# Add and GELU on one core: GpSimd instead of ScalarE waits for the last store at the program's end

## The chip, the core and the metric

The kernel runs on one core of a Trainium2 chip. The metric is the device time of one execution in microseconds, as the median of several runs. Beside the runs there is one profiled execution; its rows, clocked from the first instruction of the program, are what is read below.

## What is computed

```python
def setup_inputs():
    batch, dim = 1024, 4096
    return {
        "x": np.random.randn(batch, dim).astype(np.float32),
        "y": np.random.randn(batch, dim).astype(np.float32),
    }

def reference(x, y):
    z = x + y
    return (0.5 * z * (1 + np.tanh(np.sqrt(2 / np.pi) * (z + 0.044715 * z ** 3)))).astype(np.float32)
```

Two matrices of 16 MiB each are read, added and passed through the tanh form of GELU; one matrix of 16 MiB is written.

## The kernel before

Each of the 128 partitions holds 8 rows of 4096, which are 32768 values in a row. The loads are two of x (16384 values a partition each, L125) and four of y (8192 each, L132). All transfers are issued by SyncE (SP) on one queue. The arithmetic goes in 16 chunks of 2048: the sum z = x + y is made by GpSimd (10 chunks) or VectorE (6 chunks), both at L149; ScalarE takes the magnitude of z (L154) and the GELU of its negative (L157) into PSUM; VectorE adds max(z, 0) and writes z back (L166). Three stores of 16384, 10240 and 6144 values a partition (L136) follow the loads in SP's queue. The order on each engine is written out by hand (L173 to L209).

After the program has been compiled, two functions edit its instruction lists. `begin_early` (L9) moves the first two loads ahead of the barrier at the program's start. `wait_late` (L23) works on the last block of the program, which every program of this kind has. In that block stand, in order:

1. SP's waits for everything that is still under way (`all_done`, L30);
2. a first barrier of all five engines: each adds one to a gather semaphore, GpSimd waits for four, takes them off and releases the other four engines;
3. GpSimd's `reset`, a drain, and the clearing of the program's semaphores (`clear`, L33, issued at L47 as ranges);
4. a second barrier of the same form.

`wait_late` takes the wait for the semaphore of the last store out of SP's waits (L40 to L43), leaves that one semaphore out of the cleared ranges (L44 to L49), and appends one instruction to the very end of the block (L50 to L63): it waits until the semaphore has reached 32 (16 for the first load of y, 16 for the last store, which share it) and subtracts 32. So barriers and clearing run while the last store is still being written, and one engine waits for the store at the end. Lines of the inserted code carry the numbers L47 and, for the rest of the end block, L213 in the profile, which is the line where the program was finished.

```python
    end.append(
        mybir.InstEventSemaphore(
            name=clear.name, engine=mybir.EngineType.Activation, debug=clear.debug,
            sync_info=mybir.SyncInfo(
                on_wait=[its],
                on_update=[
```

Of the kernel before, what the change touches and what calls it, by code (L numbers as in the profile page):

```python
# [22 lines left out]
def wait_late(nc):  # L23

    body, end = (b.instructions for b in nc.main_func.blocks[1:3])
    last = [i for i in body if isinstance(i, mybir.InstDMACopy)][-1]
    (sem,) = [u.id for u in last.sync_info.on_update]
    all_done = end[0]  # L30
    reset = next(i for i in end if isinstance(i, mybir.InstDrain) and i.is_reset_sema)
    at = end.index(reset)
    clear = end[at + 1]  # L33
    first, stop = reset.reset_range_start, reset.reset_range_stop
    assert all_done.engine == mybir.EngineType.SP and reset.engine == mybir.EngineType.Pool
    assert isinstance(clear, mybir.InstISA) and clear.engine == mybir.EngineType.Pool
    waits = all_done.sync_info.on_wait
    (its,) = [w for w in waits if w.id == sem]

    end[0] = mybir.InstDrain(  # L40
        name=all_done.name, engine=all_done.engine, debug=all_done.debug, is_reset_sema=False,
        sync_info=mybir.SyncInfo(on_wait=[w for w in waits if w.id != sem], on_update=[]),
    )  # L43
    parts = []  # L44
    for f, e in ((first, sem), (sem + 1, stop)):
        if f < e:
            nc.gpsimd.sem_clear(range(f, e))  # L47
            parts.append(nc.cur_bb.bb.instructions.pop())
    end[at + 1 : at + 2] = parts  # L49
    end.append(  # L50
        mybir.InstEventSemaphore(
            name=clear.name, engine=mybir.EngineType.Activation, debug=clear.debug,
            sync_info=mybir.SyncInfo(
                on_wait=[its],
                on_update=[
                    mybir.SyncUpdate(
                        sync_type="semaphore", id=sem, ant_name=its.ant_name,
                        update_mode="sem-sub-imm", update_value=its.wait_value,
                    )
                ],  # L60
            ),
        )
    )  # L63
# [3 lines left out]
def kernel(  # L67
# [145 lines left out]
    tc.compile()  # L213
    begin_early(nc, 2)
    wait_late(nc)


# [28 lines left out]
```

## Time and profile before

| what | us |
|---|---|
| median of 3 runs | 120.06 (120.06 to 120.14) |
| span of the profiled execution, first to last instruction of the program | 118.57 (118.6 on the page) |
| median less span | 1.49 |
| last store issued by SP | 107.56 |
| its landing, issue to last of 16 completions | 11.0 |
| busy: VectorE, ScalarE, GpSimd | 59.8, 60.8, 55.5 |
| busy share of the DMA queue's packets | 98.6% of 16 engines |

The profiled execution's own device time is not among the times shown; its span and the records of semaphores around it are. The span ends with ScalarE's instruction at the end of the block. What lies after it is no part of the kernel's code: the trace has there only updates of semaphores by the frame in which every program runs, the last of them 120.18 us after the first instruction.

In the profile, an engine's name with a q (ACTq, POOLq) is its sequencer: instructions that wait, count or branch, and keep no arithmetic unit busy. Semaphore instructions are shown with the time at which their wait was met, not the time at which the wait began. An update is the moment at which a semaphore's value changes.

### The profile page before, as it was taken

The numbers are of one execution on the slowest core, as the hardware profiler recorded it, in microseconds if no ns is written. First come the engines' busy times: TensorE is split into PE (matmuls) and PEld (weight loads), VectorE is DVE, ScalarE is ACT, GpSimd is POOL, SyncE is SP. The second block draws the span as 40 slices with busy tenths as digits, with TensorE's granted clock in tenths as the row PEclk, the third lists the DMA queues.
The fourth block names the chain that finished last, engine by engine and source line by source line (L and its number), as shares of the span: only waits on it lengthen the run. The fifth ranks groups of instructions, "written<-read, shape, count | busy, mean of one in ns | idle before, by whom it ended". The sixth has DMA issues, their size and how long they took to land.

```text
span 118.6 us, 160 instructions
## 1 busy us (share of the span) xinstructions
DVE 59.8 (50%) x24; ACT 60.8 (51%) x34; POOL 55.5 (47%) x14
## 2 busy tenths in 40 slices
DVE  0000000000399999699994594257999457742000
ACT  5000000000067979999379705797798999940000
POOL 0000000000399999997000029999999999100000
DMA  7989888998889988988899898998899889999996
GB/s 243 464 365 696 354 354 354 663 398 354 354 387 497 531 354 354 707 354 354 354 420 464 365 520 354 531 531 354 354 531 531 354 354 442 442 442 442 398 398 265
DMA packets 1296, 50.33 MB, mean 424 GB/s; under 512 B 144, under 2 KB 144, under 8 KB 144
## 3 DMA queue, kind: packets, MB, share of 16 engines
q1 hardware_dynamic: 1296, 50.33, 98.6%
HBM read 33.55 MB, written 16.78 MB: 424 GB/s over the span
## 4 chain that ended last, share of the span: by engine, by line
DMA 48%; POOL 34%; POOLq 4%; ACT 3%; DVE 2%; issue 0%; SPq 0%; DVEq 0%
POOL z L149 34%; DMA z<-in_x_dram 26%; DMA y<-in_y_dram 21%; POOLq L213 4%; DVE z L166 2%; ACT w L154 2%; ACT w L157 2%; SPq L132 0%; POOLq L149 0%; DVEq L166 0%
## 5 line engine op out<-in xcount | busy, mean ns | idle before, releaser
L149 POOL TENSOR_TENSOR z<-z,y 128x2048 f32<-128x2048 f32 x10 | 55.3, 5563 | 45.6 <-DMA z<-in_x_dram 31.1
L154 ACT ACTIVATE w<-z 128x2048 f32<-128x2048 f32 x16 | 30.1, 1880 | 42.5 <-DVE z L149 36.0
L166 DVE SCALAR_TENSOR_TENSOR z<-z,w 128x2048 f32<-128x2048 f32 (+1 forms) x17 | 36.4, 2157 | 16.0 <-ACT w L157 16.0
L149 DVE TENSOR_TENSOR z<-z,y 128x2048 f32<-128x2048 f32 x6 | 24.0, 4009 | 30.3 <-DMA z<-in_x_dram 30.1
L157 ACT ACTIVATE w<-w 128x2048 f32<-128x2048 f32 x16 | 29.8, 1862 | 0.5
L198 ACT ACT_TABLE_LOAD x1 | 1.3, 1283 | 1.3 <-PEq L230 1.3
L197 DVE MEMSET one<- 128x1 f32 x1 | 0.1, 59 | 1.3 <-PEq L230 1.3
L198 ACT ACTIVATE one<-one 128x1 f32<-128x1 f32 x1 | 0.2, 203 | 0.0
L230 POOL MEMSET const-float32-0.0<- 128x1 f32 x1 | 0.1, 98 | 0.2 <-issue 0.2
L230 POOL MEMSET const-bfloat16-1.0<- 128x1 bf16 x1 | 0.1, 101 | 0.0
L230 POOL MEMSET const-uint8-127<- 128x1 uint8 x1 | 0.1, 101 | 0.0
L230 POOL MEMSET const-float32-1.0<- 128x1 f32 x1 | 0.1, 98 | 0.0
## 6 DMA issues: line engine op xcount, KB each, us to landing
y<-in_y_dram SPq DMA_DIRECT2D x4, 4096.0 KB, 23.7
out_dram<-z SPq DMA_DIRECT2D x1, 5120.0 KB, 14.9
out_dram<-z SPq DMA_DIRECT2D x1, 3072.0 KB, 11.0
z<-in_x_dram SPq DMA_DIRECT2D x2, 44.9
out_dram<-z SPq DMA_DIRECT2D x1, 21.6
```

The costliest lines, as they stand in the source:

```text
L149: eng.tensor_add(out=zt[:, a:b], in0=zt[:, a:b], in1=yt[s][:, o : o + b - a])
L154: nc.scalar.activation(out=wt[c], in_=zt[:, a:b], func=act.Abs)
L157: nc.scalar.activation(out=wt[c], in_=wt[c], func=act.Gelu_apprx_tanh, scale=-1.0)
L166: ins = nc.vector.scalar_tensor_tensor(out=zt[:, a + o : a + o + n], in0=zt[:, a + o : a + o + n], scalar=0.0, in1=wt[c][:, o : o + n], op ...
L197: nc.vector.memset(one, 0.0)
L198: nc.scalar.activation(out=one, in_=one, func=act.Gelu_apprx_tanh)
L213: tc.compile()
L230: nc = _bacc.Bacc("TRN2", target_bir_lowering=False, num_devices=1)
```

## The change

The one instruction at the end of the block is given to GpSimd instead of ScalarE. What it waits for and what it subtracts stay the same. All engines' other instructions and their order stay the same.

```diff
--- before.py
+++ after.py
@@ -49,7 +49,7 @@
     end[at + 1 : at + 2] = parts
     end.append(
         mybir.InstEventSemaphore(
-            name=clear.name, engine=mybir.EngineType.Activation, debug=clear.debug,
+            name=clear.name, engine=mybir.EngineType.Pool, debug=clear.debug,
             sync_info=mybir.SyncInfo(
                 on_wait=[its],
                 on_update=[
```

## The prediction, as it went on record

> **What bounds the kernel now.** I read the slices of the page first, then the DMA issues, then the instructions of the end block engine by engine, and last the records of semaphore updates after the span.
>
> The page's slices and its row of the queue:
>
> ```profile
> DVE  0000000000399999699994594257999457742000
> ACT  5000000000067979999379705797798999940000
> POOL 0000000000399999997000029999999999100000
> DMA  7989888998889988988899898998899889999996
> ...
> q1 hardware_dynamic: 1296, 50.33, 98.6%
> ...
> out_dram<-z SPq DMA_DIRECT2D x1, 3072.0 KB, 11.0
> ```
>
> The transfers fill the time; the compute engines have ended three slices before the end. The last store is issued at 107.56 us and takes 11.0 us, so its data are complete at about 118.5, and the span is 118.57. The end of the kernel is the landing of this store, and then whatever stands behind the one instruction that waits for it. The engine lists for the end block say which one:
>
> ```profile
> L213 ACTq EVENT_SEMAPHORE  x3: 17/17/17, 111.6 to 118.6; - x3
> L213 ACTq DRAIN  x2: 14/952/1891, 103.3 to 111.6; - x2
> ```
>
> ```profile
> L213 POOLq EVENT_SEMAPHORE  x4: 17/17/17, 111.4 to 112.1; - x4
> L213 POOLq DRAIN  x3: 34/83/21507, 79.9 to 111.9; - x3
> ```
>
> ```profile
> L47 POOLq EVENT_SEMAPHORE_RANGE_CLEAR  x2: 48/68/88, 111.7 to 111.8; - x2
> ```
>
> Durations are shortest/median/longest in ns, then the first and last start in us. ScalarE's third event instruction starts at 118.6 and ends the span. GpSimd's last one is at 112.1: it has finished its barriers and its clearing 6.4 us before the store lands. The chain of waits on the page stops at 107.5, at VectorE's last L166, since it follows compute; it is no help with the end.
>
> The trace's semaphore records continue it at finer grain. The 16 completions of the last store come between 118.075 and 118.532; ScalarE's instruction starts at 118.553, 21 ns after the sixteenth, and its subtraction is recorded at 118.577. Then semaphore 2, which the kernel doesn't use, is raised at 112.393, 118.709, .748, .791, .814, .913, .952, .986 and 119.033: nine updates, the first one long before the store has landed and the second 132 ns after ScalarE's subtraction. Between 118.932 and 119.595 some 250 semaphores are changed in five runs, and from 119.819 to 120.177 semaphore 2 is raised nine times again. I read the nine as a barrier of the frame around the program, in which the five engines post one after the other and are let go in turn: one engine had posted at 112.393, ScalarE was second and the one that all waited for, the rest followed in hops of 39, 43 and 23 ns.
>
> **The change part by part.**
>
> *The wait itself.* One EVENT_SEMAPHORE goes from ScalarE's sequencer to GpSimd's. It takes 17 ns on both (rows above). How soon it is met: at 31.353 one x load landed, and ScalarE's waiting instruction started at 31.374, GpSimd's at 31.377. That is 21 against 24 ns: plus 0.003 us. Nothing of the program is queued behind it on GpSimd; ahead of it GpSimd's end work ends at 112.08, so the wait begins 6.4 us before it is met, and that work stays covered by the store. If that cover were gone, with a store that landed at 112, the end block's 0.7 us (111.40 to 112.08) would show, before as after. SP's queue and the DMAs are not touched; GpSimd issues none.
>
> *The hop.* ScalarE now posts early, as soon as the engine ahead of it has. All wait for GpSimd instead. If GpSimd is third in the chain, the hop of 39 ns from second to third leaves the path: minus 0.039. The records name no poster. I take third because the next hop (43 ns) is the slowest and fits VectorE, whose event instructions take 21 ns where ScalarE's, GpSimd's and SP's take 17, and because the first engine's 223 ns fits TensorE: its last own update is at 112.170, and the first post of the second round comes 224 ns after the last of the slow reset run. The bounds: were GpSimd fifth, three hops leave the path, minus 0.105 (39 + 43 + 23); were it first, one more is added, plus 0.039.
>
> *GpSimd's step from its subtraction to its post.* For ScalarE it is 132 ns. For GpSimd the trace doesn't show it: it arrived somewhere between 112.08 and 118.71, under cover. From below: two event instructions in a row on GpSimd start 79 ns apart (111.429 and 111.508), so hardly less than 79. From above: if GpSimd is the engine that posted at 112.393, 314 ns after its last update at 112.079. The nearest row is the start of the program, where the same frame hands over to it: in the barrier just before, updates six to nine are at -0.122, -0.084, -0.050 and -0.003; with the order taken above these are SP, VectorE, GpSimd and ScalarE. ScalarE's first instruction is at 0.129, which is 132 ns after its update, the same 132 as at the end; GpSimd's is at 0.131, which is 181 ns after. I take 181: plus 0.049. GpSimd's drains support a value above ScalarE's: 34 ns is the shortest against 14 (rows above).
>
> *The sum.* 0.003 - 0.039 + 0.049 = plus 0.013 us. Against the profiled execution: its path from the last landing to the second round of posts grows by 13 ns, and the span's own last row, now GpSimd's, stays at about 118.58. What lies behind (resets and second barrier, 119.03 to 120.18) keeps its length, since the run of resets that ends last (119.595, the others by 119.39) belongs to neither engine by the order above. The profiled execution's own time isn't listed; I carry the difference over to the median, 120.06, and get **120.07**.
>
> The Trainium skill has a rule for the hop ("Runtime: NRT & Kernel Launch", section "The ~15µs preamble/postamble breakdown"): the barrier around a program goes as a serpentine through the five engines, at 44 ns a hop and eight hops. The hops recorded here are 23 to 47 ns with one of 99, so rule and trace agree in form. With 44 for 39 the sum would be plus 0.008 us by it, 120.07 as well. The same section gives 1.5 us for the barrier after the kernel and 1.5 us for the reset behind it, an estimate of 3 us together, where the records here have 0.89 us from ScalarE's post to the last reset (118.709 to 119.595); the measurement decides.
>
> **The rivals.**
>
> *GpSimd has end work of its own that is hidden today (slower).* Between GpSimd's last update and its post the frame may have it do more than ScalarE: stop its cores, reset its configuration. Today up to 6.6 us of it would be unseen (112.08 to 118.71); after the change all of it follows the landing. For it: in the barrier at the start of the program, recorded from -8.325, the third post came at -2.700, 0.87 us after the second (-3.574), so an engine that I take for GpSimd arrives last there. Against it: no transfer and no other semaphore is recorded between 112.4 and 118.0. It decides once GpSimd's step is longer than 0.41 us, which is 0.132 + 0.039 + 0.24. Priced by the start's 0.87 us it gives 120.06 + 0.003 - 0.039 + 0.87 = 120.89; a part of it gives 120.31 upward.
>
> *GpSimd posts first.* Then its step is 314 ns, and it is one hop further from the end: 0.003 + 0.039 + 0.182 = plus 0.224, 120.28, still within 0.2%. Against it stands the 224 ns of the second round, which repeats TensorE's 223.
>
> *The change shortens the chain.* GpSimd fifth with a step of 79 ns: 0.003 - 0.105 - 0.053 = minus 0.155, 119.90. A gain of more than 0.2% needs the whole of ScalarE's 132 ns and all three hops to vanish (minus 0.237), or something that the records after the span don't show, such as an end of ScalarE alone within the 1.49 us that lie between span and median. Time 119.8 or less.
>
> *The change does nothing*, since the store's landing is what everybody waits for: that is the forecast in all but 13 ns.
>
> **How the numbers follow.** 0.2% of 120.06 is 0.24 us, about what a measurement of this kernel can tell from no change; the runs shown differ by 0.08. Chances: the forecast, GpSimd third with a step between 79 and some 240 ns, 119.95 to 120.17: 0.55. GpSimd first, 120.28: 0.09. A shorter chain within 0.2%, down to 119.85: 0.04. Hidden end work of more than 0.24 us: 0.25. Faster by more than 0.2%: 0.07. So faster 0.07, same 0.68, slower 0.25. The range goes from 119.93 (the step of 79 ns in third place, minus 0.089, and 0.04 for the spread of runs) to 120.50, which takes in over half of the hidden work's case; the rest of it, the faster case and most of the shorter chain's are left out, together some 0.2. The likeliest case's own range is 119.95 to 120.17.
>
> **What would show it.** In the profile after: ScalarE's event instructions in the end block end at 112.1 (two, not three), GpSimd has a fifth at about 118.6, and the span stays within 0.1 us of 118.6. In the semaphore records: two posts of semaphore 2 near 112.4, then seven from about 118.76 on. If just one stands there early, GpSimd is first or ScalarE's place was read wrongly. If the next post comes over 0.41 us after GpSimd's subtraction, the hidden work is real. I am wrong if the median leaves 119.82 to 120.30, above all if it does so with the span unchanged.

## The result, and the profile after

| | before | after |
|---|---|---|
| median of 22 runs each, us | 120.15 | 120.48 |
| ratio to before, 95% interval | | 1.0024 (1.0015 to 1.0033) |
| span of the profiled execution, us | 118.57 | 118.62 |
| median less span, us | 1.58 | 1.86 |

The changed kernel is slower by a quarter of a per cent, 0.29 us by the ratio (0.18 to 0.40). The page shows none of it. The slices, the queue's row and the last store of the changed kernel, to be laid beside those shown of before:

```profile
DVE  0000000000499999699994594257999457752000
ACT  5000000000067979999379705797798999940000
POOL 0000000000399999997000039999999999100000
DMA  8989888988899988988899998998898889999996
...
q1 hardware_dynamic: 1296, 50.33, 98.7%
...
out_dram<-z SPq DMA_DIRECT2D x1, 3072.0 KB, 11.1
```

The transfers are as full as before, and the store takes 11.06 us from issue to landing, against 10.97. It lands at 118.582 instead of 118.532, and the loss is counted from the landing below. The end block's rows of the changed kernel, ScalarE and then GpSimd (duration in ns, shortest/median/longest, then first and last start in us):

```profile
L213 ACTq EVENT_SEMAPHORE  x2: 17/17/17, 111.5 to 112.1; - x2
```

```profile
L213 POOLq EVENT_SEMAPHORE  x5: 17/17/17, 111.4 to 118.6; - x5
L213 POOLq DRAIN  x3: 34/82/21526, 79.8 to 111.9; - x3
```

```profile
L47 POOLq EVENT_SEMAPHORE_RANGE_CLEAR  x2: 48/68/88, 111.7 to 111.8; - x2
```

The one instruction has moved, and the rest of the end block is where it was. So the loss must lie behind the span, and there the trace has only its records of semaphore updates. They are no rows of the page. Here they are for both kernels, in us from the first instruction; a post is one update of semaphore 2, counted from the end block on:

```
                                    before     after
last of the store's 16 completions  118.532    118.582
subtraction of 32                   118.577    118.631
semaphore 2, 1st post               112.393    112.366
             2nd                    118.709    112.400
             3rd                    118.748    119.184
             4th                    118.791    119.228
             5th                    118.814    119.252
             9th                    119.033    119.470
             18th and last          120.177    120.615
landing to last record              1.645      2.033
```

After the change two posts are early instead of one, so GpSimd is third among the engines that post. From its subtraction to its post 0.553 us go by; ScalarE's took 0.132. From the third post on the two columns run in step: 1.429 us to the last record in before, 1.431 after. The difference from landing to last record, which I call the tail, is 0.388 us, inside the interval of the runs.

### The profile page after: what moved, and what is told of

Read it like the earlier page. It is cut to its first block, busy times and chain, and to the rows that moved or that the text cites. A ratio compares the mean times of both kernels' runs of the same rounds, so it can differ in the third digit from the quotient of the medians.

```text
span 118.6 us, 160 instructions
## 1 busy us (share of the span) xinstructions
DVE 59.8 (50%) x24; ACT 60.8 (51%) x34; POOL 55.5 (47%) x14
## 4 chain that ended last, share of the span: by engine, by line
DMA 47%; POOL 34%; POOLq 4%; ACT 3%; DVE 2%; issue 0%; SPq 0%; DVEq 0%
POOL z L149 34%; DMA z<-in_x_dram 26%; DMA y<-in_y_dram 21%; POOLq L213 4%; DVE z L166 2%; ACT w L154 2%; ACT w L157 2%; SPq L132 0%; POOLq L149 0%; DVEq L166 0%
## 5 line engine op out<-in xcount | busy, mean ns | idle before, releaser
L149 POOL TENSOR_TENSOR z<-z,y 128x2048 f32<-128x2048 f32 x10 | 55.3, 5559 | 45.6 <-DMA z<-in_x_dram 31.0
L149 DVE TENSOR_TENSOR z<-z,y 128x2048 f32<-128x2048 f32 x6 | 24.0, 4012 | 30.3 <-DMA z<-in_x_dram 30.0
```

Of the source, the lines that this page charges most:

```text
L149: eng.tensor_add(out=zt[:, a:b], in0=zt[:, a:b], in1=yt[s][:, o : o + b - a])
```

## The experiments

Two theories were to be told apart. **Theory 1**: each engine has a step of its own between the program's last instruction and its post in the frame's barrier, and GpSimd's is 0.55 us. **Theory 2**: the 0.55 us are a price of waking from a long wait, which engines other than ScalarE, or GpSimd alone, would pay at any last instruction that waits for the store. The first three experiments change one word of the kernel before, the engine of the inserted instruction.

**VectorE waits.**

```diff
-            name=clear.name, engine=mybir.EngineType.Activation, debug=clear.debug,
+            name=clear.name, engine=mybir.EngineType.DVE, debug=clear.debug,
```

> VectorE instead of ScalarE waits for the last store and subtracts. Theory 1 (after its last instruction, each engine has a step of its own up to its post in the frame's barrier, GpSimd's 0.55 us, ScalarE's 0.13, and the posts go in the order TensorE, ScalarE, GpSimd, VectorE, SyncE): three posts of semaphore 2 stand near 112.4 us, the next comes some 0.20 us after VectorE's subtraction (VectorE took 204 ns from its release to its first instruction at the program's start). Against before: +0.204 -0.132 -0.039 -0.043, minus 0.01 us, ratio 1.000. Theory 2 (ScalarE is the exception, any other engine that wakes from a long wait needs some 0.5 us): the next post comes some 0.5 us after the subtraction, plus 0.3 us or 1.0025.

120.07 us against 120.08, ratio 0.9994 (0.9983 to 1.0006; brackets hold the 95% interval). VectorE's and GpSimd's rows in this kernel's end block:

```profile
L213 DVEq EVENT_SEMAPHORE  x3: 21/21/21, 111.9 to 118.9; - x3
```

```profile
L213 POOLq EVENT_SEMAPHORE  x4: 17/17/17, 111.8 to 112.4; - x4
```

VectorE's third event instruction stands at the end, GpSimd is back at four. Three posts come early: 112.781, 112.816 and 113.021. The third is the one that the records of before hid: GpSimd's last update is at 112.467, and its post follows 0.554 us later, here without any long wait on GpSimd. VectorE posts 0.174 us after its subtraction. Theory 1 holds in kind and size; theory 2's plus 0.3 us is not there.

**SyncE waits.**

```diff
-            name=clear.name, engine=mybir.EngineType.Activation, debug=clear.debug,
+            name=clear.name, engine=mybir.EngineType.SP, debug=clear.debug,
```

> SyncE waits for the last store and subtracts. Theory 1: four posts stand near 112.4 us, the fifth comes some 0.12 us after SyncE's subtraction (122 ns from its release to its first instruction at the start). Against before: 0.122 -0.132 -0.039 -0.043 -0.023, minus 0.115 us, ratio 0.9990. Theory 2: the fifth post comes some 0.5 us after the subtraction; plus 0.26 us, 1.002.

119.89 us against 120.08, ratio 0.9975 (0.9961 to 0.9988). SyncE's row:

```profile
L213 SPq EVENT_SEMAPHORE  x7: 17/17/28, 108.7 to 119.3; - x7
```

Four posts are early (113.163, .198, .403, .446); the next record of semaphore 2 comes 0.140 us after SyncE's subtraction. From landing to last record 1.484 us, 0.161 less than before. The gain is larger than the 0.115 expected, though SyncE's step is 18 ns longer than the 122 taken: its subtraction is recorded 34 ns after the landing where ScalarE's needs 45, and in the chain the hop behind the fifth post, which I read as SyncE's turn and which takes 99 ns in before, is 43 here. This version beats both kernels. Theory 2 is excluded again.

**TensorE waits.**

```diff
-            name=clear.name, engine=mybir.EngineType.Activation, debug=clear.debug,
+            name=clear.name, engine=mybir.EngineType.PE, debug=clear.debug,
```

> TensorE waits for the last store and subtracts. Theory 1: no post of semaphore 2 before the store has landed; the first comes 0.22 us after TensorE's subtraction (223 ns after its last update in before), the second 0.034 us later. Against before: 0.223 +0.034 -0.132, plus 0.125 us, ratio 1.001. Theory 2: the first post comes some 0.5 us after the subtraction; plus 0.4 us, 1.0034.

120.34 us against 120.08, ratio 1.0019 (1.0005 to 1.0034). TensorE's row (its sequencer is listed with the weight loads, PEld):

```profile
L213 PEldq EVENT_SEMAPHORE  x3: 51/51/51, 111.7 to 118.7; - x3
```

Its event instructions take 51 ns, three times the 17 of ScalarE, GpSimd and SyncE. No post is early; the first comes at 119.038, 0.267 us after the subtraction, and the others follow. So TensorE is first, and the order of the chain is settled: TensorE, ScalarE, GpSimd, VectorE, SyncE. Landing to last record is 1.860 us, plus 0.215 where plus 0.125 was expected: the step is 267 ns instead of 223, and the subtraction comes 91 ns after the landing instead of 45. Theory 2's step of some 0.5 us isn't there either.

**GpSimd's last instruction is split.** In the changed kernel the inserted instruction keeps only its wait, and behind it come

```diff
+    end.append(
+        mybir.InstDrain(
+            name="I-900001", engine=pool, debug=clear.debug, is_reset_sema=False,
+            sync_info=mybir.SyncInfo(on_wait=[], on_update=[]),
+        )
+    )
+    end.append(
+        mybir.InstEventSemaphore(
+            name="I-900002", engine=pool, debug=clear.debug,
...
+                        update_mode="sem-sub-imm", update_value=its.wait_value,
```

> As in the changed kernel, but GpSimd's last instruction is split in three: an event instruction that only waits, a drain, an event instruction that subtracts. Theory 1 (the 0.55 us belong to what the frame has GpSimd do after its last instruction): drain and subtraction follow the wait within 0.2 us, the drain takes under 0.1 us, and the post comes 0.55 us after the subtraction as before; the time is the changed kernel's plus 0.15 to 0.2, so about plus 0.5 us or 1.004 against before. Theory 2 (waking from the long wait costs): the drain starts, or ends, some 0.4 us late, the post comes within 0.2 us of the subtraction, and the time is the changed kernel's plus 0.1 at most, 1.003.

120.48 us against 120.08, ratio 1.0029 (1.0016 to 1.0042). GpSimd's rows (the end block is L226 in this kernel):

```profile
L226 POOLq EVENT_SEMAPHORE  x5: 17/17/17, 111.4 to 118.7; - x5
L226 POOLq DRAIN  x4: 34/58/21514, 79.9 to 118.6; - x4
```

One more drain than in the changed kernel, and still five event instructions: the one that only waits has been merged into the drain, which carries the wait in the trace. The drain starts 24 ns after the landing and takes 34 ns, the subtraction is recorded at 118.685, 89 ns after the drain's start, and the post follows 0.553 us after that. So GpSimd is quick right after the wait, and the 0.55 us begin behind the program's last instruction. The size was off: two instructions in place of one cost 0.065 us (2.098 from landing to last record against 2.033), not 0.15 to 0.2.

**GpSimd without arithmetic.** The changed kernel, with all sums on VectorE:

```diff
-    by_dve = {0: 0, 2: 0, 4: 2, 6: 4, 8: 8, 12: 10}
+    by_dve = {k: max(0, k - 1) for k in range(C)}
```

> GpSimd waits at the end as in the changed kernel, but it does no arithmetic: all 16 sums are made by VectorE, one chunk ahead, and its two configuration instructions of L149 are gone. Only the step from GpSimd's subtraction to its post is read. Theory 1a (the frame's end work on GpSimd is the same whatever ran): 0.55 us. Theory 1b (it is the price of having used its cores or loaded their configuration): near what the other engines show, 0.13 to 0.27 us. The kernel's own time should stay within some 1 us, since the transfers set it.

A single run gave 120.77 us against 120.13. The busy times and VectorE's groups show the moved sums, and GpSimd's end rows have lost the drain of 21.5 us that waited for them:

```profile
DVE 70.9 (60%) x34; ACT 61.3 (52%) x34; POOL 0.2 (0%) x4
...
L149 DVE TENSOR_TENSOR z<-z,y 128x2048 f32<-128x2048 f32 x16 | 36.5, 2286 | 34.1 <-DMA z<-in_x_dram 30.1 <-DMA y<-in_y_dram 4.0
```

```profile
L213 POOLq EVENT_SEMAPHORE  x5: 17/17/17, 111.6 to 118.7; - x5
L213 POOLq DRAIN  x3: 34/41/70, 1.2 to 112.0; - x3
```

The subtraction is at 118.757 and GpSimd's post at 119.311: 0.554 us. It is theory 1a: neither the sums nor the configuration that L149 loads (two MODIFY_POOL_CONFIG instructions of 11 ns in the other kernels, none here) have a part in it. What this kernel leaves on GpSimd are four small memsets at the start, so a price of any use at all is not excluded. The profile of this kernel has a hop of 0.192 us in the second round of posts (third to fourth) where the others have 0.043 to 0.045, and so its tail, 2.183 us, is not to be compared. One profile doesn't tell why.

**The end block left as it was made.**

```diff
     begin_early(nc, 2)
-    wait_late(nc)
```

> The end block is left as it was made (no wait_late): SyncE waits for the last store too, and both barriers and the clearing come after it. If GpSimd's 0.55 us also stand at the end of an ordinary program: from the landing 0.02 us to SyncE, 0.80 us of end block (111.274 to 112.079 in before), 0.55 us to GpSimd's post, 1.43 us from there to the last record (119.184 to 120.615 in the changed kernel), 2.81 us, against 1.64 in before: plus 1.16 us, ratio 1.0097; the first two posts come before GpSimd's, which is third and stands 0.55 us after its last update. If the 0.55 us come only where GpSimd's last instruction has waited long for a transfer: GpSimd posts as soon as the second post is there, 0.035 + 0.039 us after the first, and the sum is 2.64 us, plus 1.00, ratio 1.0083.

121.19 us against 120.13, ratio 1.0094 (1.0077 to 1.0111). SyncE's and GpSimd's rows:

```profile
L213 SPq EVENT_SEMAPHORE  x6: 17/28/7267, 107.9 to 119.2; - x6
```

```profile
L213 POOLq EVENT_SEMAPHORE  x4: 17/17/17, 118.6 to 119.2; - x4
```

One of SyncE's event instructions, a wait for two semaphores, now lasts 7267 ns, until the store has landed, and GpSimd's four come after it. It is listed from 111.245, just after the first of its two semaphores is complete at 111.229: for a wait on two, the listed start is not the time at which the whole wait was met. GpSimd's last update is at 119.221, the first two posts are at 119.535 and 119.569, and GpSimd's at 119.774, again 0.553 us after its update and 0.205 us after the second post, where a hop that nobody holds up takes 0.039. So GpSimd's step also sets the end of this program when it doesn't wait late. Landing to last record is 2.715 us, plus 1.070 against before. Some 0.1 us less than expected, since landing to GpSimd's last update takes 0.732 us here: one range is cleared instead of two.

All comparable tails together, from the profiled executions, with the ratios times the median of before for comparison (all in us):

| who waits | subtraction to next post | landing to last record | less before's 1.645 | runs, us against before (95%) |
|---|---|---|---|---|
| SyncE | 0.140 | 1.484 | -0.161 | -0.30 (-0.47 to -0.14) |
| VectorE | 0.174 | 1.618 | -0.027 | -0.07 (-0.20 to 0.07) |
| ScalarE (before) | 0.132 | 1.645 | | |
| TensorE | 0.267 | 1.860 | 0.215 | 0.23 (0.06 to 0.41) |
| GpSimd (after) | 0.553 | 2.033 | 0.388 | 0.29 (0.18 to 0.40) |
| GpSimd, split | 0.553 | 2.098 | 0.453 | 0.35 (0.19 to 0.50) |
| SyncE, ahead of the end block | | 2.715 | 1.070 | 1.13 (0.92 to 1.33) |

The records account for the runs in every line, within the intervals. In each of the profiles of this table the stretch from the ninth post to the last is the same, 1.144 to 1.146 us.

## Why the prediction had the right map and too small a sum

The forecast was plus 0.013 us; the records show plus 0.388 and the runs plus 0.29 (0.18 to 0.40). The prediction named as the sign of being wrong a median outside 119.82 to 120.30, above all with the span unchanged, and that is what came: 120.48, with spans of 118.57 and 118.62. So its likeliest case failed.

**What bounds the kernel: right.** The end is the landing of the last store and what stands behind it; the stretch behind the landing holds the whole difference, 0.388 us in the records.

**The wait, plus 0.003 us: right.** GpSimd's instruction starts at 118.606, 24 ns after the landing at 118.582, as its row at 31.377 had shown; ScalarE's needed 21.

**The hop, minus 0.039 us: right.** GpSimd is third. The order of posts, read from the speeds of hops and steps, is borne out engine by engine.

**GpSimd's step, plus 0.049 us: wrong, and this is the step that failed.** It was taken as 181 ns, from the time between GpSimd's release and its first instruction at the program's start. It measures 553. The row was chosen because ScalarE's was 132 ns at both ends of the program. That agreement was no evidence for GpSimd: what the frame has an engine do ahead of the program and behind it need not be the same. For TensorE, too, the same row, with 315 ns from the last update of the barrier to its first instruction, is not the 267 of the end. The upper bound of the step was wrong as well. The text had 314 ns, by assuming GpSimd to be the first to post, while its forecast has GpSimd third. For that place the trace of before only said that GpSimd was ready at some time before 118.71, which leaves 6.6 us open, and the forecast's own upper end should have come from there.

**What lies behind: right.** From the third post to the last record 1.429 us before and 1.431 after.

**The first rival happened**, end work of GpSimd that the store had hidden, with a chance of 0.25. Its condition, a step of over 0.41 us, was met. Its price was too high. The 0.87 us from the start's barrier isn't a constant: in the profile of the changed kernel the third post there comes 0.505 us after the second (-3.288 to -2.783), and over all eight profiles the gap goes from 0.505 to 1.278, while the step at the end stays at 0.553 or 0.554. And the sum that gives 120.89 adds the whole 0.87, where the forecast and the condition of 0.41 count a step less ScalarE's 0.132; in those terms it would have been 120.76. The argument against it, that no transfer and no other semaphore is recorded while GpSimd was out of sight, was worth little, because its 0.55 us leave no such record when they are in full sight either. With the step of 0.553 the sum of the prediction would have been 0.003 - 0.039 + 0.421 = plus 0.385 us, against 0.388 in the records. The time of 120.48 us lies at the upper edge of the stated range, and outside the likeliest case's own. That the range holds it is no merit of the sum: the upper end was set to take in a part of this rival. And some 0.09 us of the way from 120.06 to 120.48 are no effect of the change, since the median of before in the same comparison is 120.15. Whether the loss is above the 0.2% that the prediction drew as its line (0.24 us) the runs leave open; the records put it above.

**Not settled:** what GpSimd does in its 0.55 us. It is not woken late, by the one profile without them it has nothing to do with its sums or their loaded configuration, and the profile shows no instruction and no transfer there. Why the hop that I read as SyncE's turn takes 43 ns rather than 99 when all others have already posted wasn't tried either.

The second round of posts, in which only the first post has to be waited for, takes 358 ns in before and 357 after (119.819 to 120.177, 120.258 to 120.615). The Trainium skill ("Runtime: NRT & Kernel Launch", section "The ~15µs preamble/postamble breakdown") puts the pass of the barrier ahead of a kernel through the five engines at about 355 ns, and the round recorded here behind the kernel agrees. What decides in this case is not this pass but the engines' own steps up to their posts, 0.132 us against 0.553.

## What to carry to other kernels

When the last thing in a program is a transfer, choose who waits for it by what that engine still has to do afterwards, and by its place in the closing barrier: here SyncE is cheapest and GpSimd dearest, with 1.484 and 2.033 us from the landing to the last record. An engine that finishes early hides its end work, so a trace in which it was never late gives no price for it; take the whole hidden stretch as the upper bound, or measure it by making an engine late that comes behind it in the barrier, as VectorE did here for GpSimd. A loss that the span doesn't show can still be read from semaphore records behind it.

## What the runs showed of the hardware

GpSimd's step from its last update to its post is 0.553 or 0.554 us in the six profiles that show it, whether it ran the sums or not and whether it had waited for the store or not. The other engines' steps are 0.13 to 0.27 us. The same event instruction takes 17 ns on ScalarE, GpSimd and SyncE, 21 on VectorE and 51 on TensorE. The end is 1.07 us longer when the two barriers, the clearing and GpSimd's step stand behind the last store than when they run under it and ScalarE alone waits.
